# Low halves of the attention stage's weights by ScalarE and an accumulating transfer, and probabilities scaled by one product

## The chip, the cores and the metric

The kernel runs on one core of a Trainium2 chip, with 1 of its 8 cores in use. The time is device microseconds of one execution. All inputs lie in the chip's memory and are float32; the result is a 512 x 1024 float32 array. The engines are TensorE (PE; its weight loads are PEld), VectorE (DVE), ScalarE (ACT), GpSimd (POOL) and SyncE (SP), which issues most transfers.

## What is computed

The reference chains two transformer blocks over 512 positions of width 1024: a hybrid mixer, a cross attention and a gated feed-forward, then an attention-and-pooling mixer (here "the attention stage"), an MLP, a gated linear attention and a second MLP. The stage that the change touches, cut to what matters:

```python
def nsa_pool_mixer(x, w_in, cmp_pos, cmp_w1, cmp_b1, cmp_w2, pool_w, pool_scale, w_out):
    h = x @ w_in                       # queries of 8 heads, 6 key/value sets, gates, pooled part u
    gates = jax.nn.sigmoid(h[..., o2:o3])
    ...
    o_c = softmax(qb @ kc, block mask) @ vc        # compressed keys
    o_s = softmax(qb @ k_sel, causal) @ v_sel      # selected blocks (at this length: all of them)
    o_w = softmax(qb @ k_w, causal window) @ v_w   # window (at this length: all earlier positions)
    o = gb[..., 0:1] * o_c + gb[..., 1:2] * o_s + gb[..., 2:3] * o_w
    ...
    o_pool = pool_mixer(u, pool_w, pool_scale)     # means over 2, 4, 8, 16 positions, then a matrix
    return jnp.concatenate([o_nsa, o_pool], axis=-1) @ w_out
```

## The kernel before

Every large product is made in a split precision: an operand x is kept as a high half (x rounded to the matmul's format) and a low half (x minus the high half), and one product is three matmuls, hi·hi, hi·lo and lo·hi (`mm`). So each weight tile, a **unit** of 128 x 1024 floats, is loaded by SyncE into a raw buffer `wr` (pool `wp`, `N_RAW` = 5 buffers, line 33), and `wunit` (line 644) makes two pages of it, `wh` and `wl`, in two parts of 512 columns: ScalarE copies raw to `wh` and VectorE subtracts, `wl = wr - wh`. There is a second way in `wunit`, taken by units 9 to 23 of the program (line 654), all of them in the first mixer: ScalarE writes `wl = -wh`, and when both parts are done one transfer, issued by GpSimd, adds the whole raw tile to `wl` (line 663).

The program is not written in the order in which it runs. `Recorder` takes down every operation; some have several forms, each on another engine (`either`: VectorE or GpSimd). `Plan` (line 224 on) then schedules all of them with costs written in `price1`: it takes at each step the operation that can start first, by priority, and of several forms the one that finishes earliest; a load of unit k waits in the plan for the last use of unit k-5 (line 275). Eight more rounds with priorities taken from the plan's end are tried and the best plan of the model is kept. The plan fixes the order of each engine's queue; on the chip an engine goes through its queue in that order, and waits only for data and for buffers. In the planner's books a buffer is free when the last instruction that uses it has ended; a GpSimd transfer counts there as 1.2 us on GpSimd with another 5.2 us until its data may be used. Where TensorE would stand over 1 us in the plan, filler matmuls on the identity are put in (`emit`).

The attention stage is `nsa` (line 1507). It compresses keys (`compress`), makes keys, values and the first queries (`keys`, `queries(0)`, `values_in`), and then goes four times (b = 0..3, two heads each) through: `cmp_attn` on the compressed keys, four `scores` (two heads g, two key sets s), the next queries and one `pool` branch in between, and the product with the values, gathered in one bank. In `scores` (line 1713), for each of four blocks of 128 positions: score matmuls and mask into a bank, the negated maximum (VectorE), exp with its sum (ScalarE, tile `p`), the sum's reciprocal (VectorE, tile `sm`), the scaling of `p` by reciprocal and gate (line 1732, VectorE or GpSimd), transposes on TensorE, and the split of the result into `pt` (ScalarE copies, VectorE subtracts). `pool` runs its shifted sums on GpSimd (tile `nx`). After the loop come `pool_out`, then the output projection in two halves: `proj_n` on the pool part (tile `pool`) and `proj_n_steps` on the attention part (tile `o`), with four units each. The stage's weight units are, in order of recording: 3 for compress(0), 1 for keys(0), 3 for compress(1), 1 for keys(1), 1 for queries(0), 4 for values_in, then three query units and four pool units in the loop, one of 512 columns for pool_out, and four plus four for the output projection.

All instructions are emitted at line 523, so the profile's groups are told apart by tile names.

Of the kernel before, what the change touches and what calls it, by code (L numbers as in the profile page):

```python
# [11 lines left out]
AF = mybir.ActivationFunctionType  # L12
OP = mybir.AluOpType
# [79 lines left out]
class Engine:  # L93
    def __init__(self, rec, name):
        self.rec, self.name = rec, name
# [451 lines left out]
class Block:  # L547
    def __init__(self, ctx, tc, a, out):
        self.tc, self.a, self.out = tc, a, out
        self.nc = Recorder(tc.nc)  # L550
        self.n = 0
        E = ctx.enter_context
        self.const = E(tc.tile_pool(name="const", bufs=1))
        self.wp = E(tc.tile_pool(name="wp", bufs=N_RAW))
        self.pgp = E(tc.tile_pool(name="pgp", bufs=N_PAGE))
        self.s2p = E(tc.tile_pool(name="s2p", bufs=N_HALF))
        self.small = E(tc.tile_pool(name="small", bufs=1))
        self.psp = E(tc.tile_pool(name="psp", bufs=8, space=PSUM))
        self.rules(5)
        self.early = 0  # L560
        self.x = self.const.tile([P, NT, D], F32, name="x")

    def uid(self, s):
# [80 lines left out]
    def wunit(self, loads, n=1024):  # L644

        nc = self.nc
        raw = self.wp.tile([P, 1024], F32, tag="wr", name=self.uid("wr"))
        hi, lo = self.page("wh"), self.page("wl")
        firsts = []
        for view, src in loads:  # L650
            firsts.append(len(nc.ops))
            nc.sync.dma_start(view(raw), src)
        nc.units.append((firsts, hi.tensor.name, self.quota))
        add = 9 <= len(nc.units) < 24 and len(nc.units) % 1 == 0
        for c in ((0, 512), (512, n)) if n > 512 else ((0, n),):
            c = slice(*c)
            if add:
                nc.scalar.activation(hi[:, c], raw[:, c], AF.Copy)
                nc.scalar.activation(lo[:, c], hi[:, c].bitcast(F32), AF.Copy, scale=-1.0)
            else:  # L660
                self.split(hi[:, c], lo[:, c], raw[:, c], weights=True)
        if add:
            nc.gpsimd.dma_start(out=lo[:, :n], in_=raw[:, :n], accum_op=OP.add)
        return Split(hi, lo)
# [842 lines left out]
    def nsa(self, xT):  # L1507
        nc, a = self.nc, self.a
# [17 lines left out]
        gates = misc[:, 128:224].rearrange("p (i c) -> p i c", c=24)  # L1526
# [83 lines left out]
        def queries(b):  # L1610
            u = self.wunit([(lambda r, g=g: r.rearrange("p (k g c) -> p k g c", g=2, c=64)[:, :, g, :],
                             w[:, g * 256 + b * 64:g * 256 + b * 64 + 64].rearrange("(k p) c -> p k c", p=P))
                            for g in range(2)])
            ps = self.proj_t(u.map(lambda t: t.rearrange("p (k c) -> p k c", c=P)), xT)
            t = self.page("q")
            q = [t[:, g * 512:(g + 1) * 512] for g in range(2)]
            for g in range(2):
                stack(q[g], ps, g, 0.125)
            return q
# [4 lines left out]
        def values_in():  # L1624
            pss = [self.ps() for _ in range(NT)]
            for k2 in range(4):
                r0 = k2 * 256
                wr = lambda c0, c1: w[r0:r0 + 256, c0:c1].rearrange("(k p) c -> p k c", p=P)
                v = lambda r: r[:, :560].rearrange("p (k c) -> p k c", c=280)
                u = self.wunit([(lambda r: v(r)[:, :, 0:128], wr(896, 1024)),  # L1630
                                (lambda r: v(r)[:, :, 128:280], wr(1152, 1304))], 560)
                for i in range(NT):
                    for kk in range(2):
                        k = k2 * 2 + kk
                        self.mm(pss[i][:, :280], xT[k][:, i * P:(i + 1) * P], u[:, kk * 280:(kk + 1) * 280],
                                k == 0, k == 7)
            for s in range(2):
                vst[s] = self.page("v").rearrange("p (g i e) -> p g i e", g=2, e=P)
            for i in range(NT):
                for s in range(2):  # L1640
                    src = pss[i][:, s * 128:(s + 1) * 128].rearrange("p (g e) -> p g e", e=64)
                    self.split(vst[s][:, :, i, 0:64], vst[s][:, :, i, 64:128], src)
                nc.scalar.activation(gates[:, i, :], pss[i][:, 256:280], AF.Sigmoid)
# [69 lines left out]
        def scores(b, g, s, q):  # L1713

            t0, t1 = self.page("pt"), [self.page("pt") for _ in range(2)]
            t0 = [t0[:, h * 512:(h + 1) * 512].rearrange("p (i j t) -> p i j t", i=2, t=P) for h in range(2)]
            t1 = [t.rearrange("p (i j t) -> p i j t", i=2, t=P) for t in t1]
            for i in range(NT):
                n = (i + 1) * P
                ps = self.ps()  # L1720
                with nc.together():
                    for j, k in enumerate((kst[s, g].hi, kst[s, g].lo)):
                        nc.tensor.matmul(ps[:, :n], q[:, i * P:(i + 1) * P], k[:, :n], start=j == 0, stop=False)
                    nc.tensor.matmul(ps[:, i * P:n], self.identr, self.mnegr, start=False, stop=True)
                nm = self.sm([P, 1])
                nc.vector.tensor_reduce(nm, ps[:, :n], axis=AX.X, op=OP.max, negate=True)
                p = self.s2("p")
                sm = self.sm([P, 1])
                nc.scalar.activation(p[:, :n], ps[:, :n], AF.Exp, bias=nm, accum_out=sm)
                nc.vector.reciprocal(sm, sm)  # L1730
                gi = (g * 4 + b) * 3 + 1 + s
                self.either("tensor_scalar", p[:, :n], p[:, :n], sm, gates[:, i, gi:gi + 1], op0=OP.mult, op1=OP.mult)
                pp = self.ps()
                self.turn(pp, [p[:, j * P:(j + 1) * P] for j in range(i + 1)])
                hi, lo = (t[:, i % 2, 0:i + 1, :] for t in (t0, t1)[i // 2])
                self.split(hi, lo, pp[:, :n].rearrange("p (j t) -> p j t", t=P))
            return t0, t1
# [5 lines left out]
        keys(1)  # L1743
        q = queries(0)
        values_in()
        for b in range(4):
            o = self.pair("o")
            of = self.s2("of")
            nq = None
            pc = cmp_attn(b, q)  # L1750
            for g in range(2):
                ts = []
                for s in range(2):
                    ts.append(scores(b, g, s, q[g]))
                    if s == 0 and g == 0 and b < 3:
                        nq = queries(b + 1)
                    if s == 0 and g == 1:
                        pool(b)
                po = self.ps(True)
                nc.tensor.matmul(po, vcst[:, g, :], pc, start=True, stop=False)  # L1760
                for s in range(2):
                    for half in range(2):
                        for j in range(2 + 2 * half):
                            i0 = max(0, j - 2 * half)
                            c = slice((2 * half + i0) * P, (2 * half + 2) * P)
                            with nc.together():
                                for h in range(2):
                                    nc.tensor.matmul(po[:, c], vst[s][:, g, j, :], ts[s][half][h][:, i0:2, j, :],
                                                     start=False, stop=s * half * h == 1 and j == 3)
                t = self.s2("t")[0:64, :]  # L1770
                nc.scalar.activation(t, po[64:128, :], AF.Copy)
                nc.vector.tensor_add(of[64 * g:64 * g + 64, :], po[0:64, :], t)
            self.split(o.hi, o.lo, of)
            oT.append(o)
            q = nq
# [4 lines left out]
        us = [self.wunit([(lambda r, g=g: r[g * 64:(g + 1) * 64, :],  # L1780
                           wo[g * 256 + b * 64:g * 256 + b * 64 + 64, :]) for g in range(2)])
              for b in range(4)]
        return self.proj_n_steps(oT, None, 0, None, us)

    def gla(self, xT):
# [254 lines left out]
```

## Time and profile before

| what | value |
|---|---|
| median of 3 runs | 1894.33 us (1893.68 to 1895.68) |
| the profiled execution | 1896.43 us, its span 1894.7 us |
| PE busy | 1863.6 us (98%) |
| DVE busy | 1441.0 us (76%) |
| ACT busy | 976.2 us (52%) |
| POOL busy | 83.4 us (4%) |
| the chain that ended last | PE 85%, DVE 10%, ACT 2% |

The span is the time from the first to the last instruction in the profiled execution; the 1.7 us around it are start and end. Busy times of different engines overlap. A matmul's record lasts longer than the step to the next one, since matmuls are pipelined; the step is read from a stretch that holds only one kind. The attention stage lies at 740 to 972 us of the span: the part ahead of its loop to 810, the loop to 926, the output projection to 972.

### The profile page before, as it was taken

Reading aid. Unit: us, or ns where it says so; the run is one execution under the profiler, and the core shown is the slowest. Engines: PE = TensorE matmul, PEld = TensorE weight load, DVE = VectorE, ACT = ScalarE, POOL = GpSimd, SP = SyncE. Lnnn points to the kernel's source line nnn. Section 1 sums busy time; section 2 is a strip of 40 time slices with the busy share of each in tenths; the row PEclk is TensorE's granted clock in tenths of the full one; section 3 lists DMA queues with packets and bytes.
Section 4 is the critical chain, followed back from the end, with each engine's and each line's share of the span. In section 5 each row is a group of like instructions: output and inputs, shape, how many; then the busy total and the mean of one; then the engine's idle time right before and its main releaser. Section 6 shows DMA issues by size and latency. Waiting matters only on the chain.

```text
span 1894.7 us, 27250 instructions
## 1 busy us (share of the span) xinstructions
PE 1863.6 (98%) x10076; PEld 1592.5 (84%) x10076; DVE 1441.0 (76%) x3154; ACT 976.2 (52%) x1943; POOL 83.4 (4%) x128
## 2 busy tenths in 40 slices
PE   9999999999999999999999999999999999999997
PEld 8889788798888888888888888888999988888886
DVE  8998574675677688589886878779575687778687
ACT  5787354363443343577645545443575446455440
POOL 0120000000000000012200000000000000000001
PEclk9999999999999999999999999999999999999999
DMA  7654421431341453311422333342232332333231
GB/s 232 133 135 141 149 79 34 112 111 46 95 117 46 132 146 64 84 42 34 123 79 67 89 112 100 116 139 63 78 91 81 90 97 66 93 98 123 89 123 45
DMA packets 217631, 184.28 MB, mean 97 GB/s; under 512 B 25414, under 2 KB 194826, under 8 KB 217498
## 3 DMA queue, kind: packets, MB, share of 16 engines
q1 hardware_dynamic: 215338, 175.66, 31.9%
q0 software_dynamic: 2160, 6.88, 2.1%
q8 instruction: 79, 1.29, 0.3%
q14 instruction: 54, 0.44, 0.1%
HBM read 173.54 MB, written 2.10 MB: 93 GB/s over the span
## 4 chain that ended last, share of the span: by engine, by line
PE 85%; DVE 10%; ACT 2%; issue 1%; DMA 1%; POOL 0%; DVEq 0%; ACTq 0%; POOLq 0%; SPq 0%
PE ps L523 85%; DVE sm L523 2%; DVE wl L523 1%; DVE gcv L523 1%; DVE x L523 1%; DVE xtl L523 1%; DMA wr<-in_w_in_dram 1%; DVE pt L523 0%; DMA wr<-in_w_up_dram 0%; ACT p L523 0%; DVE gs L523 0%; DVE p L523 0%; DMA wl<-wr 0%; ACT xth L523 0%; DVE nat L523 0%
## 5 line engine op out<-in xcount | busy, mean ns | idle before, releaser
L523 PE MATMUL ps<-xth,wh 128*128 128x512 f32 (+1 forms) x1464 | 516.6, 353 | 1.8 <-DVE cs L523 1.8
L523 PE MATMUL ps<-xtl,wh 128*128 128x512 f32 (+1 forms) x1464 | 514.2, 351 | 1.3 <-DVE xtl L523 1.2
L523 PE MATMUL ps<-xth,wl 128*128 128x512 f32 (+1 forms) x1464 | 514.1, 351 | 0.6 <-DVE wl L523 0.6
L523 DVE TENSOR_TENSOR wl<-wr,wh 128x512 fp32r<-128x512 f32 x470 | 305.0, 681 | 92.0 <-PE ps L523 36.9
L523 ACT ACTIVATE wh<-wr 128x512 fp32r<-128x512 f32 (+2 forms) x497 | 281.2, 622 | 106.6 <-PE ps L523 48.1
L523 PEld LDWEIGHTS ps<-xth,wh 128*128 128x128 f32 x1464 | 276.2, 189 | 41.5 <-ACT sc L523 1.9
L523 PEld LDWEIGHTS ps<-xtl,wh 128*128 128x128 f32 x1464 | 276.1, 189 | 41.3 <-DVE xtl L523 2.1
L523 PEld LDWEIGHTS ps<-xth,wl 128*128 128x128 f32 x1464 | 275.7, 188 | 40.6 <-DVE wl L523 1.4
L523 PE MATMUL ps<-wq,qd 128*128 128x512 f32 x1152 | 281.4, 393 | 0.1
L523 PEld LDWEIGHTS ps<-wq,qd 128*128 128x128 f32 x1152 | 216.4, 188 | 50.7 <-DVE wq L523 1.0
L523 ACT ACTIVATE wq<-wr 128x512 fp32r<-128x512 f32 x224 | 135.6, 624 | 110.7 <-PE ps L523 64.3
L523 DVE TENSOR_TENSOR wq<-wr,wq 128x512 fp32r<-128x512 f32 x224 | 149.2, 684 | 37.0 <-ACT wq L523 36.3
L523 DVE TENSOR_TENSOR x<-x,ps 128x512 f32<-128x512 f32 (+1 forms) x182 | 122.0, 676 | 43.9 <-PE ps L523 43.5
L523 PE MATMUL ps<-wh,hid 128*128 128x512 f32 (+1 forms) x368 | 112.2, 383 | 0.0
L523 ACT ACTIVATE r<-ps 128x512 f32<-128x512 f32 x64 | 37.9, 592 | 112.3 <-PE ps L523 112.3
L523 PE MATMUL ps<-wh,xth 128*128 128x256 f32 (+2 forms) x320 | 94.6, 296 | 0.0
L523 PE MATMUL ps<-wl,xth 128*128 128x256 f32 (+2 forms) x320 | 94.0, 294 | 0.0
L523 PE MATMUL ps<-wh,xtl 128*128 128x256 f32 (+2 forms) x320 | 93.9, 293 | 0.0
L523 PEld LDWEIGHTS ps<-wh,hid 128*128 128x128 f32 x368 | 68.0, 188 | 14.6
L523 DVE TENSOR_TENSOR acc<-acc,ps 128x512 f32<-128x512 f32 x104 | 69.3, 680 | 8.2 <-PE ps L523 8.2
L523 PE MATMUL ps<-wl,hid 128*128 128x512 f32 (+1 forms) x184 | 70.5, 383 | 0.0
L523 DVE TENSOR_TENSOR wr<-wr,wr 128x512 f32<-128x512 f32 x96 | 65.0, 684 | 3.3 <-DMA wr<-in_mlp_w_dram 2.9
(384 smaller groups left out, 3011.9 us busy)
## 6 DMA issues: line engine op xcount, KB each, us to landing
wr<-in_mlp_w_dram SPq DMA_DIRECT2D x128, 512.0 KB, 3.6
wr<-in_w_up_dram SPq DMA_DIRECT2D x44, 512.0 KB, 4.0
wr<-in_c_w_in_dram SPq DMA_DIRECT2D x24, 512.0 KB, 3.8
wr<-in_w_down_dram SPq DMA_DIRECT2D x22, 512.0 KB, 3.6
wr<-in_w_in_dram SPq DMA_DIRECT2D x16, 512.0 KB, 5.5
wr<-in_w_xkv_dram SPq DMA_DIRECT2D x16, 512.0 KB, 6.7
wl<-wr POOLq DMA_DIRECT2D x12, 512.0 KB, 5.1
wr<-in_w_out_dram SPq DMA_DIRECT2D x8, 512.0 KB, 3.5
```

The lines of the kernel that those rows point to most:

```text
L523: getattr(getattr(self.rec.nc, eng), method)(*args, **kw)
```

## The change

Three edits, all for the attention stage.

- A flag `adding` is set after `values_in()` and cleared at the stage's end. While it is set, every unit made by `wunit` takes the second way: ScalarE writes `wh` and then `wl = -wh`, and a GpSimd transfer adds the raw tile. This holds for 16 units: queries 1 to 3, the four pool units, pool_out and the eight of the output projection.
- In `scores`, the reciprocal `sm` is multiplied by the gate's column first (a 128 x 1 product on VectorE), and `p` is scaled by that one column.
- The scaling of `p` has three forms: ScalarE (a copy with a scale), GpSimd and VectorE (with one scalar). Before it had two, VectorE and GpSimd, with two scalars.

```diff
@@ class Block, __init__
         self.early = 0
+        self.adding = False
@@ wunit
-        add = 9 <= len(nc.units) < 24 and len(nc.units) % 1 == 0
+        add = self.adding or 9 <= len(nc.units) < 24 and len(nc.units) % 1 == 0
@@ nsa, scores
                 nc.vector.reciprocal(sm, sm)
                 gi = (g * 4 + b) * 3 + 1 + s
-                self.either("tensor_scalar", p[:, :n], p[:, :n], sm, gates[:, i, gi:gi + 1], op0=OP.mult, op1=OP.mult)
+                nc.vector.tensor_mul(sm, sm, gates[:, i, gi:gi + 1])
+                v = p[:, :n]
+                nc.add([[("scalar", "activation", (v, v, AF.Copy), dict(scale=sm))],
+                        [("gpsimd", "tensor_scalar", (v, v, sm, None), dict(op0=OP.mult))],
+                        [("vector", "tensor_scalar", (v, v, sm, None), dict(op0=OP.mult))]])
                 pp = self.ps()
@@ nsa, the loop
         values_in()
+        self.adding = True
         for b in range(4):
...
               for b in range(4)]
+        self.adding = False
         return self.proj_n_steps(oT, None, 0, None, us)
```

## Rows read from the trace of the kernel before

**Rows 1.** The page's first part: busy us, share of the span, instructions

```profile
PE 1863.6 (98%) x10076; PEld 1592.5 (84%) x10076; DVE 1441.0 (76%) x3154; ACT 976.2 (52%) x1943; POOL 83.4 (4%) x128
```

**Rows 2.** Stretches: start:end, us, busy us of each engine (instructions), granted clock, DMA share, GB/s

```profile
785.00:810.00 25.00, 22.53 (x141) 20.39 (x140) 16.17 (x43) 17.89 (x38) 0.00 (x0) 0.93 0.51 106
810.00:926.00 116.00, 113.51 (x751) 100.42 (x751) 106.83 (x312) 84.46 (x242) 29.06 (x44) 1.00 0.17 45
915.00:930.00 15.00, 15.00 (x84) 12.89 (x83) 13.66 (x23) 9.89 (x18) 5.71 (x8) 1.00 0.89 208
...
1100.00:1200.00 100.00, 100.00 (x434) 81.21 (x433) 79.00 (x139) 51.82 (x93) 1.47 (x3) 1.00 0.34 101
755.60:760.60 5.00, 5.00 (x44) 5.00 (x43) 2.14 (x6) 1.19 (x2) 0.00 (x0) 1.00 0.00 0
971.90:973.50 1.60, 1.60 (x17) 1.60 (x15) 1.43 (x3) 1.59 (x5) 0.00 (x0) 1.00 1.20 319
```

**Rows 3.** Groups on PE, 810 to 926: count, busy us, mean ns, idle before

```profile
L523 PE MATMUL ps<-k,q 128*128 128x256 f32 (+3 forms) x124 | 32.2, 345 | 0.9 <-ACT p L523 0.4 <-DVE v L523 0.3
L523 PE MATMUL ps<-pt,v 128*128 128x256 f32 x192 | 28.9, 285 | 0.0
L523 PE MATMUL ps<-ident,p 128*128 128x128 f32 x160 | 28.0, 281 | 1.6 <-DVE pt L523 0.7 <-ACT p L523 0.6 <-DVE p L523 0.3
L523 PE MATMUL ps<-xth,wh 128*128 128x512 f32 x48 | 19.3, 402 | 0.0
...
L523 PE MATMUL ps<-mnegr,ident 128*128 128x128 f32 x62 | 14.6, 236 | 0.0
...
L523 PE MATMUL ps<-kcv,q 128*128 128x64 f32 x24 | 3.2, 277 | 0.0
L523 PE MATMUL ps<-ident,cs 128*64 128x128 f32 x16 | 2.4, 272 | 0.0
...
L523 PE MATMUL ps<-ident 128*128 128x512 f32 x5 | 1.4, 404 | 0.0
```

**Rows 4.** The chain that ended last, 850 to 880: shares by line

```profile
by line: PE ps L523 23.5%; DVE sm L523 23.2%; DVE pt L523 18.8%; DVE p L523 9.0%; ACT p L523 4.9%; DVE cs L523 4.7%; ACT q L523 3.6%; issue 2.7%; DVE of L523 2.3%; DVE pct L523 2.3%; DVE r L523 2.3%; DVE rs L523 2.0%; DVE o L523 2.0%; ACTq 
```

**Rows 5.** Timeline of PE, 791 to 795: start, us, instruction, idle before

```profile
792.05 0.28 PE L523 MATMUL ps<-ident,cs 66*128 66x66 f32 x1 [0.68 <-DVE k L523]
794.12 0.76 PE L523 MATMUL ps<-xth,wh 128*128 128x512 f32 x1 [1.79 <-DVE cs L523]
```

**Rows 6.** Groups on DVE, 810 to 926

```profile
L523 DVE TENSOR_SCALAR p<-p,sm,misc 128x512 f32<-128x512 f32 (+3 forms) x38 | 16.2, 448 | 0.2
L523 DVE TENSOR_TENSOR wl<-wr,wh 128x512 fp32r<-128x512 f32 x16 | 11.0, 729 | 0.0
L523 DVE RECIPROCAL sm<-sm 128x1 f32<-128x1 f32 (+1 forms) x65 | 8.0, 152 | 0.3 <-ACT p L523 0.3
```

**Rows 7.** Groups on ACT by form, whole span

```profile
L523 ACT ACTIVATE wl<-wh 128x512 fp32r<-128x512 f32 x24 | 14.0, 645 | 0.0
...
L523 ACT ACTIVATE nat<-x,sm 128x512 f32<-128x512 f32 x12 | 8.0, 715 | 4.1 <-DVE sm L523 4.1
```

**Rows 8.** Tile wl, 30 to 170: issues (ns min/median/max) and landing

```profile
L523 POOL DMA_DIRECT2D wl<-wr x15: 862/877/1199, 42.7 to 154.0; - x15
...
DMA to landing us min/median/max: 3.0/4.9/9.0
```

**Rows 9.** Timeline of SP's queue, 914 to 945

```profile
926.55 7.17 SPq L523 DMA_DIRECT2D wr<-in_a_w_out_dram  x4
```

**Rows 10.** Tile wl, 905 to 975: ns min/median/max, first and last start

```profile
L523 PE MATMUL ps<-wl,o x32: 387/393/398, 941.5 to 971.4; 128*128 128x512 f32 x32
```

**Rows 11.** Groups on DVE by form, whole span

```profile
L523 DVE TENSOR_SCALAR p<-p,sm,misc 128x512 f32<-128x512 f32 x14 | 7.5, 536 | 0.0
...
L523 DVE TENSOR_SCALAR p<-p,sm 128x256 f32<-128x256 f32 x16 | 4.9, 349 | 0.2
...
L523 DVE TENSOR_SCALAR p<-p,sm,misc 128x256 f32<-128x256 f32 x10 | 4.1, 406 | 0.0
```

## The prediction

> **What bounds the kernel now.** I read the page first, then the stretches, then TensorE's own groups in the attention loop, then the chain there. The page's engine line [rows 1] has TensorE busy 98% of the span, so this change can only gain where TensorE stands or runs slowly inside its own stage. The stretches [rows 2] put that stage's loop at 810 to 926 us: TensorE 113.5 of 116 us, VectorE 106.8, ScalarE 84.5, GpSimd 29.1. Busy is not the whole story, because matmuls overlap: one of 512 columns reads 393 ns, yet 434 of them fill 100 us, so 0.230 us each. In the same way 0.119 us is one of 256 columns (44 touch 5.0 us, two or three of them only at its edges), and 0.11 one of 128.
>
> So I count what TensorE has to do in the loop [rows 3]. The 144 projection matmuls of 512 columns (three rows of 48, one shown) take 33.1 us. The 124 score matmuls are 31 of each width (128 to 512): 31 x (0.230 + 0.174 + 0.119 + 0.11) = 19.6. The 192 value matmuls, 128 of 256 columns and 64 of 128 by the code's loops: 22.3. The 222 transposes and masks: 24.4. That is 682 of the 751; the other 69 are, by their names, some 44 short ones (4.8) and some 25 of 512 (5.8, of which five, 1.2 us, are the planner's filler in a gap). Sum 110.0, so about 6 us of standing plus 1.2 us of filler: **the loop holds some 7.2 us that any relief could give back**, and no more. The groups' idle shows 2.5 us openly: 1.3 released by VectorE (pt 0.7, p 0.3, v 0.3), 1.0 by ScalarE's p.
>
> Who makes it wait is seen in the chain [rows 4]: in a typical 30 us of the loop VectorE has some 60% of it (sm 23.2, pt 18.8, p 9.0 and smaller ones), TensorE 23.5%. VectorE and TensorE are nearly level, and a lighter VectorE is worth something, up to those 7.2 us.
>
> Ahead of the loop, at 785 to 810 us, TensorE stands 0.68 and 1.79 us [rows 5] and the granted clock is 0.93 [rows 2], which means that 7% x 25 x 2 = 3.5 us ran at 1.2 GHz and cost 1.75. Together 4.2 us, behind VectorE's k and cs.
>
> **Part 1: the low halves.** From the second query unit on, 16 units change: three query, four pool, pool_out (512 columns) and eight of the output projection, so 31 half splits. VectorE loses 31 subtractions, 11.0/16 = 0.69 us each in the loop [rows 6]: 21.4 us. ScalarE gains 31 negated copies of 14.0/24 = 0.58 us [rows 7]: 18.1 us. GpSimd gains 16 issues of 0.88 us [rows 8]: 14 us, in an engine that is 25% busy. Half of it falls in the loop (16 subtractions there), half in 926 to 972, where TensorE is never idle.
>
> The new wait is GpSimd's: the issue stands in its queue until ScalarE's negated copy is done, and behind it are the pool branch's shifted sums and whatever scalings of p went to GpSimd. In the loop both have other matmuls as cover, so I cost it at nothing; without that cover it is 0.6 us, one ScalarE copy, per unit and at most 16 x 0.6 = 10 us on GpSimd. The transfer itself lands 3.0 to 9.0 us after issue, median 4.9 [rows 8]. For the query and pool units the weights are split tens of us ahead. It counts where output units follow each other: SyncE issues the last two units' loads (two transfers each) at 926.6 to 933.7 [rows 9], and the groups that need the last four units begin at 941.5 [rows 10]. A raw buffer (there are five) used to come free after the second subtraction; now after two more ScalarE copies, the issue and the landing, less the two subtractions: 1.16 + 0.88 + 4.9 - 1.36 = 5.6 us later. The planner frees it in its books 1.2 us after the issue starts, so the chip's loads are later than it believes. Between 0 (the pool half of the projection, 96 matmuls or 22 us, can go first) and 5.6 us; I take 0.5, near the lower end, because TensorE has those 22 us to do.
>
> Here VectorE and GpSimd meet. The issues of the first stage, made beside a VectorE as loaded, took 862 to 1199 ns [rows 8]: at worst 0.34 us late, 16 x 0.34 = 5.4 us on GpSimd, none of it on the path. The Trainium skill (SBUF — State Buffer, "Who interferes with whom") speaks against the change: VectorE operations such as a scaling can take the port pair that it shares with GpSimd, and GpSimd, which writes this kind of transfer's descriptors, then blocks fully. By that page landings like the slowest would be common, which is rival B's time below; by the row 4.9 is the median beside a VectorE that busy, and the sum goes by the row.
>
> **Part 2: the scaling.** Each of 64 probabilities gets one more 128x1 product on VectorE: at 8.0/65 = 0.12 us as the reciprocals cost [rows 6], 8 us; it also lengthens exp, reciprocal, scaling, transpose by about 0.15 us, the mean of one [rows 6]. VectorE's scalings (38 of 64 in the loop) get one scalar less: 406 to 349 ns at 256 columns [rows 11], 38 x 0.057 = 2.2 us back. Scaling may now also go to ScalarE, where a scaled copy of 512 columns takes 715 ns [rows 7] against VectorE's 536 [rows 11]. The planner takes the earliest finisher; ScalarE is 73% busy, GpSimd mostly idle, so I take a third of VectorE's 38, about 13, moved: 13 x 0.43 = 5.6 us more off VectorE, some 6.5 us onto ScalarE. Bounds: none, and all (16 us).
>
> **The sum.** VectorE in the loop: 106.8 - 11.0 + 8 - 2.2 - 5.6 = 96 us of 116. ScalarE: 84.5 + 16 x 0.58 + 6.5 = 100. Neither is full, but ScalarE now sits where VectorE sat. Of the 7.2 us I give VectorE's share of the open idle, 1.3/2.3 = 57%, 4.1 us, less 1.1 us for the longer chain where nothing covers it (the loop's first and last softmaxes, some seven in a row at 0.15): **3.0 us**. The hand-over takes 0.5. The entry changes by 0 (its waits are on k and cs, which the change leaves; bounds -4.2 and +1.75, a second stretch at half clock). Net -2.5 us: the profiled execution, 1896.43 us with a span of 1894.7, goes to 1893.9, and the median of the runs, 2.1 us below it, to **1891.8**. Every order is planned anew over the whole program, which no row prices.
>
> **The rivals.** A, *all of it comes back*: VectorE was the only reason; the loop's 7.2 us go, hand-over free: 1887.1, and 1882.9 with the entry. For it: VectorE's 60% of the chain. Against: 1.0 of 2.3 us of open idle is ScalarE's, which gets more work. B, *the hand-over breaks, slower*: raw buffers are held 5.6 us longer, and between 915 and 930 us the DMA engines are 0.89 busy already [rows 2], so the transfers land like the slowest, 9.0 instead of 4.9: 5.6 + 4.1 = 9.7 us, less the loop's 3.0: 1901.0. It decides once the last unit's low half is later than the 22 us of pool matmuls can hide. C, *ScalarE becomes the bound*: exps queue behind negated copies, its 1.0 us of open idle doubles and more and VectorE's gain is eaten: 1894.3 to 1897. D, *the scaling stays on VectorE*, with no form on ScalarE taken: 5.6 us stay there, 0.15 us more per chain: about 1893, within the forecast's own range.
>
> **How the numbers follow.** This kernel's measurement tells some 0.2%, 3.8 us, from no change. Forecast (with D) 0.45, its own range 1889 to 1895; A 0.26; B 0.18; C 0.11. Faster: A and a fifth of the forecast, 0.35. Slower: B and a quarter of C, 0.21. Same: 0.44. The range takes most of A and the near side of B: 1885 to 1900.
>
> **What would show it.** Right: in the loop 16 fewer VectorE subtractions, VectorE under 100 us, ScalarE near 100, TensorE's 751 matmuls in about 113 us. B would show as TensorE idle at 926 to 972, released by the transfer or by a load, and loads issued 5 us later. C would show as idle released by ScalarE's p. D as no ScalarE row p<-p. If the time moves while the loop keeps its length, the new order elsewhere did it and this sum is wrong.

## The result: slower, by 16 us

The changed kernel takes 1910.97 us (median of 4 runs, 1909.14 to 1915.28) against 1895.01 (1893.68 to 1897.76) for the kernel before on the same chip: ratio 1.0084, 95% interval 1.0072 to 1.0097. The forecast was 1891.8, its range 1885 to 1900. Time, sign and range were wrong.

The profiled execution of the changed kernel took 1915.28 us, with a span of 1913.6: it is the longest of its four, 4.3 us above the median, so sizes read from it alone are somewhat large. Its page begins with this line, which answers [rows 1]: busy us, share of the span, instructions.

```profile
PE 1868.9 (98%) x10086; PEld 1596.6 (83%) x10086; DVE 1424.3 (74%) x3179; ACT 1000.4 (52%) x1993; POOL 93.0 (5%) x132
```

VectorE lost 17 us and ScalarE gained 24, as was meant. The stretches tell where the time went (start:end, us, busy us of each engine and instructions, granted clock, DMA share, GB/s); the first two answer [rows 2].

```profile
785.00:810.00 25.00, 22.63 (x134) 20.87 (x133) 13.35 (x47) 20.43 (x50) 4.73 (x5) 0.86 0.81 161
810.00:926.00 116.00, 109.77 (x727) 97.16 (x727) 97.09 (x339) 93.52 (x260) 24.89 (x30) 1.00 0.22 54
930.00:970.00 40.00, 31.11 (x129) 24.57 (x129) 15.16 (x25) 20.56 (x37) 8.99 (x13) 0.87 1.04 224
934.10:990.00 55.90, 47.02 (x191) 37.18 (x191) 28.80 (x64) 20.52 (x36) 6.62 (x8) 0.91 0.73 162
959.60:969.90 10.30, 5.25 (x12) 4.14 (x13) 2.50 (x4) 3.57 (x7) 1.32 (x2) 0.50 1.10 253
```

VectorE is at 97 us in the loop (107 before), but TensorE did 727 matmuls to 926 us, where it did 751 before. For comparison, 930 to 970 us in the kernel before:

```profile
930.00:970.00 40.00, 40.00 (x174) 32.45 (x173) 32.48 (x70) 13.67 (x24) 0.00 (x0) 1.00 0.25 70
```

To compare orders that cut the work at different times I use one measure throughout, **TensorE's idle by count**: a stretch's length, less each of its matmuls at the step at which such matmuls follow one another (0.230 us at 512 columns, and so on, as in the prediction); the planner's filler matmuls count as idle. Example: from the last product of probabilities and values (934.1 us) to the last matmul of the output projection (990.0 us) the changed kernel does 189 matmuls of 512 columns and two of 128: 55.9 - 189 x 0.230 - 2 x 0.11 = 12.2 us. The same stretch before, 926.1 to 972.0 us, gives 0.2. I call it the **hand-over**, and 810 us to the last such product the **loop**.

| idle by count, us | loop | hand-over |
|---|---|---|
| before | 7.8 | 0.2 |
| after | 14.2 | 12.2 |

The other stretches differ by -1.2 us (741 to 810 us) and +1.6 (all the rest). So the loss has two places: 12 us behind the loop, 6.4 in it. These are of one execution each; e18 below, in the same order of instructions as the changed kernel, has 8.5 and 13.6.

**The hand-over.** What TensorE waited for from 926 to 990 us (us in total, times, longest):

```profile
PE ps L523 <- DMA wl<-wr: 8.1, 2, 6.8
PE ps L523 <- ACT wh L523: 0.7, 1, 0.7
```

TensorE stands for the accumulating transfer. How that came to be late stands in SyncE's queue (start, us, instruction) and in the chain that ended last there, 930 to 966 us:

```profile
933.64 1.11 SPq L523 DMA_DIRECT2D wr<-in_a_w_out_dram  x2
936.78 0.38 SPq L523 DMA_DIRECT2D wr<-in_mlp_w_dram  x1
944.80 3.31 SPq L523 DMA_DIRECT2D wr<-in_a_w_out_dram  x4
948.39 20.59 SPq L523 DMA_DIRECT2D wr<-in_mlp_w_dram  x7
```

```profile
936.06 8.69 DMA wl<-wr
944.75 0.04 issue
...
946.60 10.04 DMA wr<-in_a_w_out_dram
...
956.70 2.48 issue
...
959.20 5.32 DMA wl<-wr
964.52 0.14 issue
964.65 1.62 PE ps L523 x3
```

One unit's transfer is issued at 936.06 and lands 8.69 us later, at 944.75; from 944.80 on SyncE issues the loads of the last two output units; the last of them is issued at 946.60 and lands 10.04 us later; ScalarE's copies take 2.5 us, the transfer 5.32, and TensorE goes on at 964.65: 28.6 us in a row, of which 24 are DMA. Before, the last two units' loads went out at 926.55 [rows 9] and, the very last, at 932.61; now at 944.80 and 946.01. That is 18 and 13 us later, not 5.6; 8 of these are the loop's own later end (934.1 for 926.1). What the loads wait for has changed. SyncE's waits from 915 to 970 us, then those of the kernel before from 905 to 945 us (us in total, times, longest):

```profile
SPq L523 <- DMA wl<-wr: 61.1, 10, 27.5
```

```profile
SPq L523 <- DVE wl L523: 67.2, 10, 25.6
```

Ten times SyncE now stands until a transfer has landed, where it stood until VectorE had subtracted. And the pool half of the projection, which should have hidden it, needs a transfer of its own and waited for that one (1.39 us at 944.79).

The transfers are also slower than where I took my median. Tile wl, 915 to 975 us, answers [rows 8] (issue ns min/median/max, then landing):

```profile
L523 POOL DMA_DIRECT2D wl<-wr x10: 862/862/958, 917.4 to 960.2; - x10
...
DMA to landing us min/median/max: 4.6/7.7/10.8
```

The issues take no longer; the landings do. The two DMA queues from 910 to 975 us (packets, MB, share of 16 engines' time) fill the DMA engines to 87%:

```profile
q1 hardware_dynamic: 9248, 7.34, 45.0%
q0 software_dynamic: 1440, 4.98, 41.4%
```

The second is the transfers: 4.98 MB took nearly the time that 7.34 MB of loads did. Finally, the granted clock falls to 0.50 (1.2 GHz) within the 6.8 us wait and stays there for 10.3 us (the last of the stretches above): 12 matmuls in 5.25 us of work are some 0.43 us each for 0.23, and 12 x 0.2 = 2.4 us are lost after the wait.

**The loop.** TensorE's idle there is in small pieces. The longest waits are on p from VectorE (2.1 us in all) and ScalarE (1.4). Another 4.6 us of the 14.2 are 20 filler matmuls (five before, 1.2 us): there the planner's own plan already had TensorE standing. Who does the scaling, 785 to 935 us (count, busy us, mean ns, idle before; VectorE's first row answers [rows 6, 11]; in this stretch of the kernel before VectorE had 39 of the 64 scalings in 16.7 us and GpSimd 25):

```profile
L523 DVE TENSOR_SCALAR p<-p,sm 128x512 f32<-128x512 f32 (+3 forms) x31 | 12.8, 421 | 0.3
L523 DVE TENSOR_TENSOR sm<-sm,misc 128x1 f32<-128x1 f32 (+1 forms) x68 | 9.8, 165 | 0.2
L523 ACT ACTIVATE p<-p,sm 128x128 f32<-128x128 f32 (+3 forms) x20 | 10.5, 538 | 1.9 <-DVE sm L523 1.5
L523 POOL TENSOR_SCALAR p<-p,sm 128x384 f32<-128x384 f32 (+3 forms) x13 | 13.8, 1067 | 70.7 <-DVE sm L523 56.3 <-ACT pt L523 9.2 <-ACT pct L523 5.2
```

ScalarE's 20 came from VectorE (8) and, more of them, from GpSimd (12). The 64 products cost VectorE some 9 us (9.8 less 0.7 for four such rows that the kernel before has too), and fewer and shorter scalings gave back 16.7 - 12.8 = 3.9.

### The profile page after: what moved, and what is told of

Same layout as the page of the kernel before. It is cut to its first block, busy times and chain, and to the rows that moved or that the text cites. A ratio compares the mean times of both kernels' runs of the same rounds, so it can differ in the third digit from the quotient of the medians.

```text
span 1913.6 us, 27403 instructions
## 1 busy us (share of the span) xinstructions
PE 1868.9 (98%) x10086; PEld 1596.6 (83%) x10086; DVE 1424.3 (74%) x3179; ACT 1000.4 (52%) x1993; POOL 93.0 (5%) x132
## 4 chain that ended last, share of the span: by engine, by line
PE 81%; DVE 10%; ACT 4%; DMA 3%; issue 2%; POOL 0%; DVEq 0%; SPq 0%; POOLq 0%; ACTq 0%
PE ps L523 81%; DVE sm L523 2%; DVE gcv L523 1%; DVE wl L523 1%; DMA wl<-wr 1%; DVE x L523 1%; DMA wr<-in_w_in_dram 1%; ACT wh L523 1%; DVE pt L523 1%; DMA wr<-in_a_w_out_dram 1%; ACT L523 0%; DMA wr<-in_mlp_w_dram 0%; DVE nat L523 0%; ACT xth L523 0%; DMA wr<-in_w_up_dram 0%
## 5 line engine op out<-in xcount | busy, mean ns | idle before, releaser
L523 DVE TENSOR_TENSOR wl<-wr,wh 128x512 fp32r<-128x512 f32 (+2 forms) x439 | 285.1, 680 | 111.2 <-ACT wh L523 54.0
L523 ACT ACTIVATE wh<-wr 128x512 fp32r<-128x512 f32 (+1 forms) x497 | 283.4, 623 | 117.3 <-PE ps L523 43.4
```

The costliest lines, as they stand in the source:

```text
L523: getattr(getattr(self.rec.nc, eng), method)(*args, **kw)
```

## The experiments

Two questions: what holds the hand-over, and why the loop got worse where VectorE got lighter. Each ratio is against runs of the kernel before on the same chip; the last two columns are idle by count in us, from one profiled execution each.

| kernel | ratio [95%] | loop | hand-over |
|---|---|---|---|
| after | 1.0084 [1.0072, 1.0097] | 14.2 | 12.2 |
| e1 part 1 alone | 1.0089 [1.0072, 1.0106] | 12.6 | 15.3 |
| e2 part 2 alone | 1.0033 [1.0021, 1.0045] | 15.3 | 0.0 |
| e3 loop's units, new scaling | 1.0018 [1.0009, 1.0027] | 12.5 | 0.1 |
| e4 output's units, old scaling | 1.0058 [1.0043, 1.0073] | 11.6 | 3.8 |
| e5 loop's units, old scaling | 0.9991 [0.9982, 1.0000] | 7.5 | 0.0 |
| e6 after, 7 raw buffers | 1.0072 [1.0059, 1.0084] | 17.3 | 7.6 |
| e7 after, buffers booked longer | 1.0084 [1.0070, 1.0098] | 14.3 | 9.6 |
| e11 after, half the bytes | 1.0055 [1.0042, 1.0067] | 14.2 | 5.1 |
| c7 before, another order | 1.0024 [1.0015, 1.0033] | 11.7 | 0.3 |
| e12 as e5, another order | 1.0017 [1.0008, 1.0026] | 10.9 | 0.0 |
| e9 as e2, number of c7 | 1.0044 [1.0031, 1.0057] | 15.7 | 0.0 |
| e10 product, no ScalarE form | 1.0019 [1.0009, 1.0028] | 11.1 | 0.1 |
| e13 part 2, no GpSimd form | 1.0017 [1.0008, 1.0026] | 12.1 | 0.2 |
| e14 as e10, two operations | 1.0005 [0.9996, 1.0014] | 9.5 | 0.1 |
| e15 as e2, two operations | 1.0036 [1.0024, 1.0049] | 14.9 | 0.0 |
| e17 as e15, product as scaling | 1.0031 [1.0018, 1.0043] | 15.1 | 0.0 |
| e18 as after, both forms | 1.0077 [1.0065, 1.0089] | 13.6 | 8.5 |
| e16 what is left | 0.9998 [0.9989, 1.0007] | 8.8 | 0.0 |

### The parts alone

**e1**: the units as in the change, the scaling as before (the new product and the three forms undone).

> Only the low halves are changed (all 16 units); the probabilities are scaled as before. Hand-over theory: five raw buffers are each held until the accumulating transfer has landed, so the loads of the output projection's units come late; this costs its 12 us here as in the changed kernel, and with the loop's part of the splits on ScalarE the time is 1906 to 1912 us. Softmax theory: the longer chain and ScalarE's scalings cost most; then this is 1894 to 1900. Replanning theory (any change of the order costs this much): no forecast, but then e1 to e4 would scatter without regard to what they contain.

**e2**: the scaling as in the change, the units as before (the attention's switch never set).

> Only the scaling of the probabilities is changed (product of gate and reciprocal, three forms); the units stay as before. Hand-over theory: 1893 to 1899 us, and no wait for a transfer between the loop and the first MLP. Softmax theory: the loop is 4 to 6 us longer as in the changed kernel, 1899 to 1905 us or more.

Part 1 alone is as slow as the whole change, and has the whole hand-over; part 2 alone has none of it, but a worse loop. The parts don't add: +16.3 and +6.1 us against +16.0 together. In e1 TensorE waits four times for a transfer, 10.3 us in all:

```profile
PE ps L523 <- DMA wl<-wr: 10.3, 4, 6.7
```

**e3** (first diff) ends the adding ahead of pool_out and the output's units; **e4** (second diff, on the old scaling) begins it there:

```
         values_in()
         self.adding = True
...
+        self.adding = False
```

```
         values_in()
-        self.adding = True
...
+        self.adding = True
```

> The flag is cleared ahead of pool_out: the seven query and pool units take the accumulating transfer, pool_out and the eight units of the output projection are split by VectorE as before; the new scaling stays. Hand-over theory: the 12 us between the loop's end and the end of the projection are gone, only the loop's 6 us can be left: 1895 to 1901 us. If the seven loop units were the cause: 1905 us and more.

> Only pool_out and the eight units of the output projection take the accumulating transfer; the loop's units and the scaling stay as before. Hand-over theory: TensorE waits for wl between the loop and the first MLP as in the changed kernel, 9 to 14 us: 1903 to 1909 us. If the seven loop units or the scaling were needed for the loss: 1893 to 1898 us.

The seven units of the loop leave no idle behind it (0.1), the nine later ones leave 3.8 (9 to 14 were expected), all sixteen 8.5 to 15.3. So the output's units are needed for the loss, and with the loop's units it is two to four times as large. That the delays of successive rounds of the five buffers add up would explain it; each of these kernels has an order of its own, so it is argued, not shown. e4 stands another 2.4 us ahead of the loop, 741 to 810 us, which the table leaves out.

### What holds the hand-over

**e6**: two more raw buffers, one fewer of two other pools.

```
-N_PAGE = 31
-N_HALF = 18
-N_RAW = 5
+N_PAGE = 30
+N_HALF = 17
+N_RAW = 7
```

> The changed kernel with seven raw buffers in place of five, paid for with one buffer fewer of two other pools. Hand-over theory (a raw buffer is held from its load to the landing of its transfer, and five of them do not cover landings of 8.7 to 10.8 us): the loads of the last units go out 5 us or more earlier, the idle between the last product of probabilities and values and the last output matmul falls from 12.2 to under 4 us, no half clock there; time 1900 to 1905. Rival (the landings themselves, or the DMA engines' total traffic, set the pace): the hand-over stays at 9 to 12 us, as the same bytes pass, time 1908 to 1912.

The hand-over is 7.6 us, between the two theories, in an order that differs throughout. But the profiled execution of e18, which has the changed kernel's order, reads 8.5, so the 12.2 is a long case, and little is left that seven buffers clearly saved; the medians' intervals overlap. With seven buffers, too, SyncE's loads waited ten times for a landing, 57.4 us in all, and the DMA engines' share from 930 to 970 us is 1.03.

**e7**: in the planner's books a raw buffer is free only after the transfer's latency.

```
-                last[t] = max(last.get(t, 0.0), end)
+                last[t] = max(last.get(t, 0.0), end + (lat if calls[0][:2] == ("gpsimd", "dma_start") else 0.0))
```

> The changed kernel, its planner told that a raw buffer comes free 5.2 us (its own latency of a GpSimd transfer) after the issue of the transfer ends and not with it. The chip's rules are the same, only the order changes. If the wait at the hand-over came from the planner's belief alone, it should now place the preparation of the units earlier or the matmuls later: hand-over under 4 us, time 1899 to 1904. If five buffers are too few whatever the order: hand-over 8 to 13 us and time 1907 to 1912. The landings of 8.7 us and more are still longer than what it is told, so a value in between speaks for the second.

Time unchanged. So it was not the planner's ignorance of the hold alone, as far as the 5.2 us that it was told can show: the landings here are longer.

**e11**: every instruction in the same order on every engine, only half the bytes of the attention's transfers. It leaves out half of the sums, so its weights aren't those of the other kernels.

```
-            nc.gpsimd.dma_start(out=lo[:, :n], in_=raw[:, :n], accum_op=OP.add)
+            m = 64 if self.adding else P
+            nc.gpsimd.dma_start(out=lo[:m, :n], in_=raw[:m, :n], accum_op=OP.add)
```

> The changed kernel, every instruction in the same order; only the accumulating transfers of the attention's fifteen later units move 64 of 128 partitions (the low half of the other 64 is left without its sum, so part of the weights is left out). Each raw buffer is still held to its transfer's landing, and the planner knows of nothing. Theory D (the DMA engines, at a share of 0.92 to 1.04 from 918 to 970 us, make the landings long): the landings at the hand-over fall from 8.7 to 10.8 us to 5 to 7 us, the hand-over's idle from 12.2 to under 5 us, the time to 1902 to 1906. Theory H (a long fixed course of each transfer through GpSimd's queue, whatever its bytes): landings of 8 us and more stay, hand-over 10 to 13 us, time 1909 to 1912. The loop's idle should stay near 14 us in both, as its order is the same.

Tile wl, 915 to 975 us:

```profile
L523 POOL DMA_DIRECT2D wl<-wr x10: 797/807/928, 916.2 to 953.2; - x10
...
DMA to landing us min/median/max: 4.6/6.2/6.6
```

No landing is above 6.6 us, the hand-over falls to 5.1 us (under 5 was expected) and the time by 5.2: theory D. Against the two executions with all the bytes, 8.5 and 12.2 us, the bytes were 3 to 7 us of it. Of the 5.1 us that stay, TensorE stands 3.2 on ScalarE's wh, behind a late load. The Trainium skill (DMA: Bandwidth & Descriptors, "Issuing engines are not separate DMA queues") says that transfers run on the same 16 DMA engines whoever starts them. The traces agree: SyncE's load took 10.04 us beside the transfers, and with half their bytes in e11 the loads' median to landing, 910 to 975 us, fell from 9.1 to 6.7.

### Why the loop got worse

**c7**: the kernel before with one number of its planner changed; the operations are the same, the order differs from the loop on.

```
-        return (0.052 if ps else 0.094) + n / 1200.0 + ...
+        return (0.053 if ps else 0.094) + n / 1200.0 + ...
```

> The kernel before, with one number of its planner changed (the fixed price of a ScalarE instruction that touches PSUM, 0.052 to 0.053 us). The list of operations is the same; what differs is the order of the attention stage, from its loop on. So nothing that the change does is in it. In the kernel before TensorE idled 7.8 us between 810 us and the last product of probabilities and values, and in the four variants so far 11.6 to 15.3 us. Theory R (any new order of the loop costs this; the order of before is a lucky one): idle of the loop 11 to 15 us, time 3 to 7 us above the kernel before. Theory P (the parts of the change cost it themselves): idle of the loop 7 to 9 us, time within 2 us of the kernel before. Both: hand-over (last such product to last output matmul) under 0.5 us.

3.9 us more idle and 4.4 us more time with nothing of the change in it (stretch as in [rows 2]):

```profile
810.00:926.00 116.00, 112.78 (x723) 98.59 (x723) 105.06 (x309) 81.68 (x238) 26.11 (x39) 0.99 0.14 38
```

**e5**: e3 with the scaling of before. **e12**: e5 with the number of c7.

> Part 1 for the seven units of the loop alone; the output projection's units by VectorE, scaling as before. It completes a square: before (neither), scaling alone (loop 15.3 us idle), loop units with the new scaling (12.5), and this. Theory R (any new order): loop 11 to 13 us, time 1898 to 1902. Theory P with the scaling as the dear part: loop 7 to 9 us, or less, as VectorE is relieved of some 8 us, and the time 1892 to 1896. Theory P with the units as the dear part: loop about 12.6 as with both halves of part 1, time 1899 to 1901. Hand-over in all cases under 0.5 us, as the output units have no transfer.

> The loop's seven units by the transfer, old scaling (the version that ran at 0.9991 of the kernel before), with the control's number in the planner: a second order of the loop with the same operations. Theory R (luck of the order, some 4 us either way): loop idle 10 to 13 us, time 1896 to 1901, so that the 1894 of the first order says little on the part. Theory P (the units' part gains in the loop): loop idle 7 to 9 us again, time 1892 to 1896.

With the planner's own number the loop idles 7.5 us (7.8 before), with the other 10.9 (11.7 in c7). So the loop's units, which take some 10 us of subtractions off VectorE, gain 0.3 to 0.8 us of idle, and the order is worth 3.4 to 3.9. e5 is 1.9 us below the kernel before, an interval that ends at 1.0000: no gain that I would claim.

**e9**: e2 with the number of c7. Its order turned out to be nearly that of e2, so it is a repeat and not a second order.

> Part 2 alone (the new scaling), with the planner's number of the control (0.053 for 0.052), so a second order of the loop with the same new operations. Idle of TensorE from 810 us to the last product of probabilities and values has been 7.5 to 12.6 us in the orders with the old scaling and 12.5 to 15.3 us in those with the new. Theory S (the new scaling costs the loop some 4 us whatever the order, as one more instruction stands between the exponential and the transposes): 12 to 16 us, time 1900 to 1904. Theory R (only the order counts): may come out as low as 8 us, time 1895 to 1899.

**e10**: e2 without the ScalarE form. **e13**: e2 without the GpSimd form.

```
-                nc.add([[("scalar", "activation", (v, v, AF.Copy), dict(scale=sm))],
-                        [("gpsimd", "tensor_scalar", (v, v, sm, None), dict(op0=OP.mult))],
+                nc.add([[("gpsimd", "tensor_scalar", (v, v, sm, None), dict(op0=OP.mult))],
```

```
-                        [("gpsimd", "tensor_scalar", (v, v, sm, None), dict(op0=OP.mult))],
```

> Part 2 alone without its ScalarE form: the product of gate and reciprocal, then the scaling by GpSimd or VectorE, as before by two engines. Theory S1 (the product, one more instruction in the chain, is what costs): loop 12 to 16 us idle, time 1899 to 1904. Theory S2 (the ScalarE form costs, as it lies in ScalarE's queue ahead of exponentials and of the units' high halves): loop 8 to 12 us, time 1895 to 1899. Theory R: anything between 8 and 15 us.

> Part 2 alone, the scaling by ScalarE or VectorE, no GpSimd form. In the runs so far GpSimd's scaling by one scalar takes 1.56 to 1.62 us at 512 columns, against 0.86 to 0.95 with gate and reciprocal as two scalars in the kernel before, and its planner prices it at 0.75. Theory A (ScalarE's form costs, as ScalarE's queue also holds the exponentials): TensorE's idle from 810 us to the last product of probabilities and values 13 to 17 us, as with all three forms (15.3), time 1900 to 1905. Theory G (GpSimd's slow form costs, whose results come later than planned): 8 to 12 us, time 1895 to 1899. With GpSimd's eleven scalings moved to the other two, a result of A may also be partly these engines' load.

Without ScalarE's form the loop idles 11.1 us, inside what the old scaling gives in its six orders (7.5 to 12.6); with all three forms 15.3. Without GpSimd's it is 12.1, between the theories' ranges, and the ratio, 1.0017, is that of e10, though ScalarE's form is still there (22 scalings). So taking away either form gives back about half of e2's loss, by medians whose intervals overlap with e2's. e10's profiled execution is also the fastest of its eleven, 3.4 us below their median, so that its 11.1 is a low case. That pointed at two suspects at once: ScalarE's form, and GpSimd's own, which has become slow: 1575 ns at 512 columns in the changed kernel where two scalars took 900. The next runs change a duration and keep every engine's order. **e14** (from e10) and **e15** (from e2):

```
-                        [("gpsimd", "tensor_scalar", (v, v, sm, None), dict(op0=OP.mult))],
+                        [("gpsimd", "tensor_scalar", (v, v, sm, 1.0), dict(op0=OP.mult, op1=OP.mult))],
```

> Product, then scaling by GpSimd or VectorE, every instruction in the same order as in the run with the product only; GpSimd's scaling is given a second factor of 1.0, so that it has two operations as before the change. Theory T (GpSimd's time hangs on the second operation): its scaling falls from 1.60 to about 0.9 us at 512 columns, TensorE's waits on GpSimd's p (1.4 us in the loop) nearly go, loop idle 11.1 to about 9.5, time 1.5 us below the product only. If the time per scaling stays at 1.6, the second scalar operand or VectorE's neighbouring work made the difference.

> Part 2 alone with all three forms, in the same order as that run; only GpSimd's scaling gets the second factor of 1.0. Theory G (GpSimd's slow form): loop idle falls from 15.3 to 12 us or less, time 1902.6 to 1899 or less. Theory A (ScalarE's form and the order that it brings): loop idle 14.5 to 15.5, time within 1 us of 1902.6, as only the 1.0 us wait on GpSimd's p at 846 us goes.

GpSimd's scaling at 512 columns in e10, then in e14:

```profile
L523 POOL TENSOR_SCALAR p<-p,sm 128x512 f32<-128x512 f32 x2 | 3.2, 1618 | 7.5 <-PE ps L523 6.1 <-DVE sm L523 1.4
```

```profile
L523 POOL TENSOR_SCALAR p<-p,sm 128x512 f32<-128x512 f32 x2 | 1.5, 745 | 7.6 <-PE ps L523 6.1 <-DVE sm L523 1.5
```

GpSimd's time hangs on the second operation, as theory T says: half the time for one more operation, and in e14 loop idle 9.5. What it is worth in the whole is not clear: the two profiled executions took the same time (1895.52 and 1895.43 us), and the medians' intervals overlap. In e15 it changes nothing (14.9, ratio as e2): theory G falls for that order, and what is left is theory A, ScalarE's form and the order that it brings. e15 and e14 differ in that form and in what the plan makes of it: 1.0036 and 1.0005, intervals apart. Form and order aren't separated. All kernels with the form idle 12.1 to 17.3 us in the loop, all without it 7.5 to 12.6: the ranges touch, and e13 has the form and loses no more time than e10 without it.

**e17** tries the last suspect, again in an unchanged order. In e2 VectorE's new 128x1 product stretched beside GpSimd's shifted sums. VectorE and GpSimd at 918 us in e2:

```profile
917.62 0.16 DVE L523 RECIPROCAL sm<-sm 128x1 f32<-128x1 f32 x1 [0.20 <-ACT p L523]
917.82 1.06 DVE L523 TENSOR_TENSOR sm<-sm,misc 128x1 f32<-128x1 f32 x1
918.90 0.68 DVE L523 TENSOR_TENSOR of<-ps,t 64x512 f32<-64x512 f32 x1
```

```profile
917.61 1.25 POOL L523 TENSOR_TENSOR nx<-nx 128x504 f32<-128x504 f32 x1
```

```
-                nc.vector.tensor_mul(sm, sm, gates[:, i, gi:gi + 1])
+                nc.vector.tensor_scalar(sm, sm, gates[:, i, gi:gi + 1], None, op0=OP.mult)
```

The rest is e15; in the planner the new form gets the product's price, which keeps the order.

> Part 2 alone with the second factor on GpSimd, in the same order; only VectorE's product of gate and reciprocal is written as a scaling by a scalar operand instead of a product of two tensors. In the run before it, the 128x1 product took 0.15 us alone but up to 1.06 us beside one of GpSimd's shifted sums (at 918 us), and TensorE stood 1.7 us on what came behind. Theory V (the two tensors of the product make VectorE wait for GpSimd): no product above 0.3 us, the waits at 914 to 922 us shrink by 2 to 3 us, loop idle from 14.9 to 12 or 13 us, time 1900 to 1901 for 1902.7. Rival (the queue's order there is at fault, the product only happens to be in it, or the other form waits as well): products still reach 0.5 us and more beside GpSimd, loop idle 14 to 15.5 us, time unchanged.

Tile sm, 810 to 925 us in e17:

```profile
L523 DVE TENSOR_SCALAR sm<-sm,misc x63: 164/204/216, 813.6 to 919.3; 128x1 f32<-128x1 f32 x63
```

The stretching is gone (216 ns at most for 1057 in e15), and time and idle stay (ratio 1.0031 for 1.0036, intervals overlapping; 15.1 for 14.9). It was real and cost no time: theory V fell. **e18** does both changes of form in the changed kernel.

> The changed kernel in its own order, with both changes of form: GpSimd's scaling with a second factor of 1.0, VectorE's product as a scaling by a scalar operand. Units as in the changed kernel. If the forms hold the loop's loss: loop idle from 14.2 to 9 to 11 us, time 1907 to 1909. If the order does: loop idle 13 to 14.5 us, time 1910 to 1911. The hand-over keeps its 12 us in both, as nothing of it is touched.

Loop idle 13.6 for 14.2, ratio 1.0077 for 1.0084 with overlapping intervals: again the two forms' durations aren't the loss, and the order with its scalings on ScalarE is what is left. The hand-over read 8.5 where 12 was expected, with nothing of it touched. The traces don't say what in these orders is bad beyond the small waits. In e2 6.7 of the loop's 15.3 us lie from 900 us on, most of it among the last softmaxes, where the granted clock is 0.85 from 910 to 922 us:

```profile
910.00:922.00 12.00, 7.99 (x49) 6.38 (x48) 9.50 (x22) 11.34 (x28) 4.88 (x8) 0.85 0.05 5
```

There ScalarE is busy 11.3 of 12 us. That its queue is what delays the last softmaxes is argued, not shown, and two runs speak against it as the only cause: from 900 us to the loop's end c7 idles some 5 us by the same count and e4 some 5.5, both with no scaling on ScalarE, where the kernel before idles some 2.

**e16**: e5, with the product and the two forms of e14.

> What is left of the change when both costs are out: the seven units of the loop by the transfer, the output units by VectorE, the product of gate and reciprocal, and the scaling by GpSimd (with a second factor of 1.0) or VectorE, without the ScalarE form. If the costs were the hand-over and the ScalarE form alone, loop idle 7 to 9 us and time 1891 to 1895, below or level with the kernel before; if the product costs too, or the order is less lucky, loop idle 10 to 13 us and time 1896 to 1899.

Loop 8.8 us, 1894.60: with the hand-over and ScalarE's form out, the rest of the change costs and gains nothing that can be measured in this one order. By c7 and e12 another order could move that by some 0.25%.

## Why the prediction was wrong, point by point

- **The reading of the loop.** The count of 7.2 us that relief could give back comes out (7.8 by the fuller count), but no kernel here gave back more than 0.3 of it. What was missing is that idle can also rise: every order is new, and c7 prices that alone at 3.9 us of idle and 4.4 of time. The prediction named it ("which no row prices") and gave it no width in the range. That is a failed step of its own.
- **The engines' sums** came out: VectorE 97.1 us for the 96 forecast, none of the 16 subtractions left in the loop; ScalarE 93.5 for 100; issues 855 to 958 ns, within [rows 8]. The step from there to time failed. VectorE's 60% of the chain [rows 4] was who happens to end last in one order, not what the loop would be without its load: e5 takes 10 us of subtractions off VectorE and gains 0.3. The 3.0 us of gain were a loss of 6.4. Another order alone loses 3.9 (c7); whether the rest hangs on ScalarE's form or on this order stays open.
- **Part 2.** "A third of VectorE's 38, about 13, moved" to ScalarE: 20 went there, 8 of them from VectorE and 12 from GpSimd. The 64 products took some 9 us for the 8 forecast. GpSimd's side was not costed at all, and its new form takes 1575 ns for 900.
- **The hand-over, the step that failed most**: "I take 0.5, near the lower end, because TensorE has those 22 us to do." It was 8.5 to 12.2. The landing was taken from the first stage's median of 4.9; here it was 7.7, up to 10.8, and 6.2 with half the bytes (e11), so that their own bytes on the loaded DMA engines are a good part of it. With 7.7 the same sum for one buffer is 8.4 us, not 5.6. The loads then stood behind the landings, ten times, and the last two units' went out 18 and 13 us later. The 22 us of pool matmuls were no cover, as they stood in the same line themselves. The seven units of the loop were held to be free, as their weights are split far ahead; alone they are (e3, 0.1), but with them the loss is 8.5 and more where e4, without them, has 3.8.
- **Rival B** is what came: TensorE idle behind the loop, released by the transfer, with late loads. Its 9.7 us of hand-over lie within the 8.5 to 12.2, in part by luck, as it counts one pass of one buffer and loads 5 us later. Its 1901.0 was still 10 us short, mostly because it took the loop's gain of 3.0 along, where the loop lost 6.4: 3.0 + 6.4 = 9.4.
- **The port rule** was weighed against the wrong instruction. GpSimd's issues were not slowed (958 ns at most at the hand-over). It was VectorE's new product that blocked, 1.06 us beside a shifted sum. The Trainium skill (SBUF — State Buffer, "Who interferes with whom") says that a VectorE instruction with two SBUF inputs contends with a GpSimd instruction that reads SBUF: the trace agrees, and by e17 it cost no time here.
- **Rivals A, C, D.** A's free gain isn't there even with the hand-over out (e5, e16). C's sign was ScalarE's p as releaser, 1.0 us before: 1.4 after, not the loss, though its thought that ScalarE's queue delays the softmaxes isn't excluded. D: ScalarE does 20 scalings, so no.
- **The entry**, forecast at 0 with bounds -4.2 and +1.75, was -1.2.

## What to carry to other kernels

Where a change holds a buffer of a ring longer, cost the hold with the landing time under the load of that stage, for every unit that goes through the ring ahead of the one that counts, and ask whether the work that is to hide it waits for the same ring. Before a part of a planned kernel is credited or blamed with a few tenths of a per cent, run the unchanged operations in another order: here that alone was 0.24%. When work is offered to a third engine, see which of the others gives it up, and what the new form takes on each.

## What was not expected of the hardware

GpSimd's scaling by one scalar takes about twice as long as with a second operation of factor 1.0, in the same order of instructions: 1618 for 745 ns at 512 columns, 1308 for 628 at 384, 928 for 506 at 256 (e10, e14). VectorE's 128x1 product of two tensors took 0.15 us alone and up to 1.06 beside a GpSimd instruction; written with a scalar operand it took 0.20, and at most 0.216 in all, beside one or not (e17).
